# A transformer layer with a state-space mixer on one core: the down projection as seven block products, with tokens on partitions

## The chip, the cores and the metric

The kernel runs on 1 core of a Trainium2 chip. TensorE (PE) multiplies, VectorE (DVE), ScalarE (ACT) and GpSimd (POOL) work on vectors, and the DMA queues of SyncE (SP), ACT and POOL move data. The metric is the device time of one execution in microseconds.

## The reference

One layer over 512 latent tokens and 256 context tokens of width 1024, all in float32. In this change only the end of the layer matters. Written with the names of the reference:

```python
out_lat = (g_ssd * (y_ssd @ w_o_ssd) + g_att * (y_att @ w_o_att)) @ w_out   # 1024 x 1024
x = x + gate1 * out_lat                       # gate1, gate2: of the six modulation vectors
h = rmsnorm(x, norm2_g) * (1 + scale2) + shift2
u = dwconv_centred(h @ w_up, conv_w, conv_b)  # 1024 x 5632, taps over 3 tokens
a, b = u[..., :2816], u[..., 2816:]
x = x + gate2 * ((silu(a) * b) @ w_down)      # 2816 x 1024
out = rmsnorm(x, final_g)
```

The six modulation vectors of 1024 come from `silu(c) @ w_mod + b_mod`.

## The kernel before

Every large product is made of three: each operand is split into a high part in the format that PE takes at full rate (`hi`, a cast on ACT, L148) and the rest (`lo`, a subtraction on DVE, L149), and PE adds hi x hi, hi x lo and lo x hi into one bank of PSUM (`gemm`, L186, products L192, L193, L195). Channels lie on partitions throughout: a weight block of 128 x 128 is the stationary operand, and 512 tokens stream past it. One "piece" is eight such blocks, 128 x 1024, 512 KB.

`run` (L166) takes the program as a list of steps with the pieces that each needs, and emits the load and split of a piece one step ahead of its use. Loads go through three raw buffers on the SP queue; split pieces have two buffers (`whi`, `wlo`). Where an output tile has only eight blocks of inputs, one piece is 24 products.

The order of instructions on each engine is drawn up when the kernel is built, from the program's order and from when an instruction's operands are expected; where `manual_schedule` names PE, PE keeps the order as written. An instruction waits in its queue until its operands are there, and all behind it wait too. DMAs that are ready early can be put far ahead of the step that they belong to.

The stages at the end, in order:

- Merge, `os_step` (L1549), eight output tiles of 48 products; the gated sum is split into `mh` and `ml`. Ten of the 32 steps `m_step` (L540) are woven in: each takes a 512 KB piece of `w_mod`, scales it by the conditioning vector on DVE (L553) and adds; after four, PE turns the sum of four column groups onto partitions (L557) and DVE reduces it into `mod2` (L559). Six more lie in the next stage, eight in the up stage.
- W_out, `out_step` (L1618) and `out_last` (L1632): eight output tiles of 24 products. The residual is added with the gate as a value per partition (L1627) and squares are added for the second norm. The last three tiles are done in halves of 256 tokens, so that the root (`half_root`, L1602; its power runs on POOL, L246) and its spreading over the partitions by PE (`rms_spread`, L249) lie beside products.
- Up, `up_step` (L1706): 22 steps of two output tiles, 48 products each. The first is done in token halves, after `norm2_k` (L1661). ACT and DVE make the convolution and the gate; the result is split into `fh` and `fl` (L1697, L1698).
- Down, `down_step` (L1743) and `down_last` (L1754): eight output tiles of 66 products over three pieces; the last tile in halves, with the sums of the final norm between them. The final scaling and the stores to `out`, channels first, end the kernel; the host transposes.

Of the kernel before, what the change touches and what calls it, by code (L numbers as in the profile page):

```python
# [44 lines left out]
def tile_hybrid_layer(  # L45
# [26 lines left out]
    sel_d: bass.AP,  # L72
    out: bass.AP,
# [12 lines left out]
    def psum_pools(**sizes):  # L86

        if banks_:
            banks_["s"].close()
        s = banks_["s"] = ExitStack()  # L90
        for name, (n, w) in sizes.items():
            pool = s.enter_context(tc.tile_pool(name="p" + name, bufs=n, space=PSUM, reuse_waits="tile"))
            banks_[name] = pool, w

    def bank(name):
        pool, w = banks_[name]
        return pool.tile([P, 512 * w], F32, tag=name, name=name)
# [8 lines left out]
    def accb():  # L106
        return bank("acc")
# [15 lines left out]
    for i in range(8):  # L123
# [5 lines left out]
        for u, n in ((0, 8), (1, 8), (2, 6)):  # L129
            src["dn", 3 * i + u] = wdn[i, :, u * 1024 : u * 1024 + n * P], n * P  # L130
# [409 lines left out]
    def m_step(i):  # L540
        cg, kk = i // 4, i % 4

        def fn(r):
# [10 lines left out]
            if kk == 3:  # L554
# [7 lines left out]
        return [("m", i)], fn  # L562
# [997 lines left out]
    x1 = [hpool.tile([P, 4, L], F32, tag=t, name="x1") for t in ("hch", "hcl")]  # L1560
    q2 = hpool.tile([P, L], F32, name="q2")
    g1h = cpool.tile([P, 8], F32, name="g1h")
    a2 = cpool.tile([P, 8], F32, name="a2")

# [3 lines left out]
    HL = L // 2  # L1568
    HALF = [slice(0, HL), slice(HL, L)]

    def add_square(q, x, o):
        if o == 0:
            S.activation(q, x, AF.Square)
        else:
            sq = tmp("tc")
            S.activation(sq, x, AF.Square)
            V.tensor_tensor(q, q, sq, ALU.add)

    def half_gemm(ps, xh, xl, z, w, m, k0, nk, after={}):

        wh, wl = w
        for k in range(m):
            n, c = k0 + k, slice(k * P, (k + 1) * P)
            h, l = xh[:, n, z], xl[:, n, z]
            T.matmul(ps[:, :HL], wh[:, c], h, start=n == 0, stop=False)
            T.matmul(ps[:, :HL], wh[:, c], l, start=False, stop=False)
            T.matmul(ps[:, :HL], wl[:, c], h, start=False, stop=n == nk - 1)
            if n in after:
                after[n]()

    def half_sums(pf, q, u):

        rms_sums(pf[:, 2 * u : 2 * u + 2], q[:, HALF[u]], 2, 0, u == 0, False)

    def half_squares(parts):
        r = []
        for n, x in enumerate(parts):
            r.append(tmp("te" if n > 1 else "tc")[:, :HL])
            S.activation(r[-1], x, AF.Square)
        return r  # L1600

    def half_root(pf, sqs, u):  # L1602
        for n, sq in enumerate(sqs):
            rms_sums(pf[:, 2 * u : 2 * u + 2], sq, 2, 0, False, n == len(sqs) - 1)
        return rms_root(pf[:, 2 * u : 2 * u + 2], 2, EPS)
# [7 lines left out]


    for o in (5, 6, 7):
        ELSEWHERE["out", o] = piece_in("yh%d" % (o - 5))

    def out_step(o):  # L1618
        def fn(w):
            xt = tmp("te")  # L1620
            nc.sync.dma_start(xt, xT[o // 2, :, (o % 2) * L : (o % 2 + 1) * L])
            ps = accb()
            gemm([(ps, mh, ml)], w)
            if o == 0:
                V.tensor_scalar_mul(g1h, mod2[:, 0:8], 0.5)
            xo = x1[o // 4][:, o % 4, :]
            V.scalar_tensor_tensor(xo, ps, g1h[:, o : o + 1], xt, ALU.mult, ALU.add)  # L1627
            add_square(q2, xo, o)

        return [("out", o)], fn  # L1630

    def out_last(*w):  # L1632
        xt = [cp.tile([P, L], F32, tag="ld", name="ld", bufs=3) for _ in range(3)]
        for i, o in enumerate((5, 6, 7)):
            nc.sync.dma_start(xt[i], xT[o // 2, :, (o % 2) * L : (o % 2 + 1) * L])
        pf = F["pf"] = misb()
        F["r2"] = []

        def root():
            F["rs2"] = half_root(pf, F["sq2"], 0)  # L1640

        def spread():
            F["r2"].append(rms_spread(F["rs2"], 2))

        with tc.manual_schedule(engines={mybir.EngineType.PE}):
            for u, z in enumerate(HALF):
                for i in range(3):
                    after = {}
                    if u == 1:
                        after = {0: {5: root}, 1: {4: spread}}.get(i, {})  # L1650
                    if i == 2:
                        after[2] = lambda u=u: half_sums(pf, q2, u)
                    ps = accb()
                    half_gemm(ps, mh, ml, z, w[i], 8, 0, 8, after)
                    x = x1[1][:, 1 + i, z]
                    V.scalar_tensor_tensor(x, ps[:, :HL], g1h[:, 5 + i : 6 + i], xt[i][:, z], ALU.mult, ALU.add)
# [249 lines left out]
```

## Time and profile before

Three runs took 1264.0, 1267.4 and 1268.2 us: a median of 1267.44. The profiled execution has a span of 1266.2 us from its first to its last instruction; its time beside the span is not listed.

| engine | busy, us | share | instructions |
|---|---|---|---|
| PE (products) | 1241.7 | 98% | 6418 |
| DVE | 871.2 | 69% | 1413 |
| ACT | 653.0 | 52% | 1221 |
| POOL | 137.5 | 11% | 113 |

Busy time of an engine is the time in which one of its instructions runs. Products on PE overlap, so the duration listed for one (0.39 us at 512 columns) is longer than the distance from one to the next. "Idle before" is the time that an engine stood still ahead of an instruction, with what ended it. Rows of DMA issues give the size and the time from issue to landing.

### The profile page before, as it was taken

How to read it: one execution, taken by the hardware profiler on the slowest of the kernel's cores; microseconds unless marked ns; L12 is line 12 of the kernel's file. 1: busy time of each engine (PE TensorE's matmuls, PEld its weight loads, DVE VectorE, ACT ScalarE, POOL GpSimd, SP SyncE). 2: the span in 40 equal slices, each digit the busy share in tenths (PEclk: the TensorE clock that was granted, in tenths of full speed). 3: DMA queues.
4: the chain of work that ended last, by engine and by line, in shares of the span. 5: the costliest groups of instructions: out<-in, count | busy, mean ns of one | idle time of the engine just before them, and what ended most of it. 6: DMA issues, size and time to landing. Idle time of an engine off the chain costs nothing.

```text
span 1266.2 us, 17234 instructions
## 1 busy us (share of the span) xinstructions
PE 1241.7 (98%) x6418; PEld 1025.9 (81%) x6418; DVE 871.2 (69%) x1413; ACT 653.0 (52%) x1221; POOL 137.5 (11%) x113
## 2 busy tenths in 40 slices
PE   7999999999999999999999999999999999999997
PEld 4698888888888778788777777889988888888886
DVE  3856887888655687877887676676777777773333
ACT  3557788877445466475674653223644444442221
POOL 0000000000000142251352530000200000000000
PEclk9999999999999999999999999999999999999998
DMA  8652242222355225345355567776233333332331
GB/s 328 245 163 86 63 133 72 88 79 76 115 161 172 92 84 150 126 136 172 109 142 175 182 218 254 235 240 200 67 115 109 125 102 115 117 112 92 99 97 67
DMA packets 90419, 174.55 MB, mean 138 GB/s; under 512 B 7648, under 2 KB 43296, under 8 KB 90336
## 3 DMA queue, kind: packets, MB, share of 16 engines
q1 hardware_dynamic: 89248, 172.41, 42.6%
q8 instruction: 50, 0.82, 0.3%
q10 hardware_dynamic: 1088, 1.05, 0.2%
q14 instruction: 33, 0.27, 0.1%
HBM read 150.82 MB, written 17.11 MB: 133 GB/s over the span
## 4 chain that ended last, share of the span: by engine, by line
PE 84%; DVE 7%; POOL 3%; ACT 2%; DMA 2%; issue 1%; SPq 0%; DVEq 0%; ACTq 0%; POOLq 0%
PE acc L195 20%; PE acc L192 20%; PE acc L193 20%; PE score L777 3%; PE po L826 3%; PE pt L813 2%; PE mis L405 2%; PE mis L1420 1%; PE mis L1414 1%; PE acc L896 1%; PE acc L898 1%; PE acc L897 1%; POOL dx L1426 1%; DVE wlo L149 1%; PE acc L1715 1%
## 5 line engine op out<-in xcount | busy, mean ns | idle before, releaser
L149 DVE TENSOR_TENSOR wlo<-wraw,whi 128x1024 fp32r<-128x1024 f32 (+1 forms) x129 | 162.4, 1259 | 122.3 <-ACT whi L148 119.0
L148 ACT CAST whi<-wraw 128x1024 fp32r<-128x1024 f32 (+1 forms) x129 | 133.1, 1034 | 185.4 <-PE acc L193 138.4
L192 PE MATMUL acc<-hlh,whi 128*128 128x512 f32 x488 | 200.1, 410 | 0.0
L195 PE MATMUL acc<-hlh,wlo 128*128 128x512 f32 x488 | 191.3, 392 | 0.0
L193 PE MATMUL acc<-hll,whi 128*128 128x512 f32 x488 | 190.9, 391 | 0.0
L192 PE MATMUL acc<-mh,whi 128*128 128x512 f32 x368 | 143.4, 390 | 0.0
L195 PE MATMUL acc<-mh,wlo 128*128 128x512 f32 x368 | 143.2, 389 | 0.0
L193 PE MATMUL acc<-ml,whi 128*128 128x512 f32 x368 | 143.2, 389 | 0.0
L195 PEld LDWEIGHTS acc<-hlh,wlo 128*128 128x128 f32 x488 | 91.6, 188 | 20.1
L193 PEld LDWEIGHTS acc<-hll,whi 128*128 128x128 f32 x488 | 91.9, 188 | 18.1 <-issue 2.4
L192 PEld LDWEIGHTS acc<-hlh,whi 128*128 128x128 f32 x488 | 91.9, 188 | 17.8 <-issue 2.4
L195 PEld LDWEIGHTS acc<-mh,wlo 128*128 128x128 f32 x368 | 69.1, 188 | 14.5
L193 PEld LDWEIGHTS acc<-ml,whi 128*128 128x128 f32 x368 | 69.1, 188 | 14.3
L192 PEld LDWEIGHTS acc<-mh,whi 128*128 128x128 f32 x368 | 69.1, 188 | 14.1
L1325 POOL TENSOR_TENSOR st<-st,eT 128x512 f32<-128x512 f32 x24 | 28.3, 1179 | 449.3 <-ACT st L1342 430.3
L246 POOL TENSOR_TENSOR rs<-ms,phalf 128x2 f32<-128x2 f32 (+1 forms) x7 | 7.4, 1051 | 543.0 <-DVE ms L245 543.0
L786 DVE CUSTOM_DVE_ANT_0 p<-score,winm,nsink 128x512 f32<-128x512 f32 (+1 forms) x64 | 51.8, 810 | 15.5 <-PE score L777 14.0
L192 PE MATMUL acc<-fh,whi 128*128 128x512 f32 x154 | 60.0, 390 | 0.0
L195 PE MATMUL acc<-fh,wlo 128*128 128x512 f32 x154 | 59.9, 389 | 0.0
L193 PE MATMUL acc<-fl,whi 128*128 128x512 f32 x154 | 59.9, 389 | 0.0
L793 ACT ACTIVATE p<-p,mneg 128x512 f32<-128x512 f32 (+1 forms) x64 | 49.7, 777 | 15.4 <-DVE mneg L786 14.8
L1207 DVE SCALAR_TENSOR_TENSOR ta<-acc,half,ta 128x511 f32<-128x511 f32 (+1 forms) x66 | 43.8, 663 | 19.6 <-ACT ta L1206 19.6
(362 smaller groups left out, 2863.5 us busy)
## 6 DMA issues: line engine op xcount, KB each, us to landing
wraw<-wup SPq DMA_DIRECT2D x44, 512.0 KB, 3.5
fb<-cs_d SPq DMA_DIRECT2D x32, 512.0 KB, 5.9
wraw<-wm SPq DMA_DIRECT2D x32, 512.0 KB, 3.6
wraw<-wx SPq DMA_DIRECT2D x24, 512.0 KB, 3.6
wm<-wm SPq DMA_DIRECT2D x16, 512.0 KB, 8.2
wraw<-wz SPq DMA_DIRECT2D x16, 512.0 KB, 3.5
wraw<-wos SPq DMA_DIRECT2D x16, 512.0 KB, 4.2
wraw<-wdn SPq DMA_DIRECT2D x16, 512.0 KB, 3.5
```

The lines of the kernel that those rows point to most:

```text
L148: S.copy(hi[:, :n], r[:, :n])
L149: V.tensor_tensor(lo[:, :n], r[:, :n], raw(hi[:, :n]), ALU.subtract)
L192: T.matmul(ps, wh, xh[:, k0 + k, :], start=a, stop=False)
L193: T.matmul(ps, wh, xl[:, k0 + k, :], start=False, stop=False)
L195: T.matmul(ps, wl, xh[:, k0 + k, :], start=False, stop=b)
L405: T.matmul(pg[i], w[a][:, i * P : (i + 1) * P], h[b], start=st and a + b == 0, stop=en and a == 1, skip_group_check=True,)
L777: T.matmul(ps[:, o : o + len(z) * P], Q[h][:, b * P : (b + 1) * P], k[:, j, z[0] * P : (z[-1] + 1) * P], start=v == 0 and o % 512 in (0, P ...
L786: V.tensor_tensor_reduce(p[:, :w], d["ps"][i][:, o0 : o0 + w], m, op0=ALU.add, op1=ALU.min, scale=1.0, scalar=nsink[:, h : h + 1], accum_o ...
L793: S.activation(p, p, AF.Exp, bias=d["mneg"][:, i : i + 1], scale=-1.0, accum_out=d["den"][:, i : i + 1])
L826: T.matmul(d["po"], vst[:, cols[x], j, :], d[y][x], start=x == 0 and y == "pth", stop=x == c - 1 and y == "ptl")
L1207: V.scalar_tensor_tensor(o[:, 1:n], ps[:, 0 : n - 1], hcol(base_w, i), o[:, 1:n], ALU.mult, ALU.add)
L1325: G.tensor_tensor(h8(n), h8(s), bc64(eT[:, z0 : z0 + 8, c]), ALU.mult)
```

## The change

The down projection becomes Strassen's method in Winograd's form on blocks of two: tokens in two halves of 256, the 2816 input channels in alternate tiles of 128 (11 pairs), the 1024 output channels in halves of 512. Seven block products take the place of eight. Each is three products per pair and token tile, now with the activations as the stationary operand and 512 output channels streaming, so the result has tokens on partitions. The inner dimension goes in two chunks, six pairs and then five.

- The sums of activations (`s3`, `r2`, `s4`, and one in place) are made on POOL by `pair_sums`, four operations of 256 columns for each pair: the first six pairs in the up stage, the other five within the down stage.
- The sums of weights are made by accumulating DMAs from POOL's queue, onto the raw piece once it has been split (`NEXT_SUM`), 24 of full or half pieces.
- Weights are split in each block product; the activations too, one pair of low halves on POOL for each on DVE. Results are saved from PSUM by ACT (`snap`), combined on DVE, multiplied by the gate, and added to the residual on POOL.
- W_out runs the same way round: all eight pieces for token tiles 0 and 1, then for 2 and 3, kept split in the buffers of the mixer's output. The gate is multiplied into the W_out piece on POOL before its split. The x rows are loaded by token into the buffers of the residual.
- Both later norms sum squares by ACT's accumulation, with the root as a value per partition. For the up projection PE turns the normed rows back (`turned`).
- The gate vectors are needed along the free dimension: their four groups are summed over partitions by a product with ones. The order of the groups is changed, and 16 of the `m_step`s lie in merge steps 2 to 6, none in the W_out stage.
- PSUM becomes one pool of eight banks from W_out on.
- The output is stored with tokens first, and the host no longer transposes.

```diff
+        if key[0] == "out":
+            G.tensor_tensor(r, r, F["g1"], ALU.mult)
...
-        cg, kk = i // 4, i % 4
+        cg, kk = (2, 3, 4, 5, 0, 1, 6, 7)[i // 4], i % 4
...
+            if kk == 3 and cg in (0, 1, 6, 7):
+                ps = misb()
+                T.matmul(ps, ones, acc, start=True, stop=True)
+                g = F["g1" if cg < 2 else "g2"][:, 512 * (cg % 2) : 512 * (cg % 2) + 512]
+                V.tensor_tensor(g, ps, g, ALU.add)
...
+    def square_sum(ss, t, c):
+        junk = tmp("tm")
+        S.activation(junk, x1_of(t, c), AF.Square, accum_out=ss[:, t, c : c + 1])
+
+    def root(ss, t):
...
+        V.tensor_tensor(ms, ss[:, t, 0:1], ss[:, t, 1:2], ALU.add)
+        V.tensor_scalar(ms, ms, 1.0 / D, EPS, ALU.mult, ALU.add)
+        G.tensor_tensor(rs, ms, phalf[:, 0:1], ALU.pow)
...
+    def out_products(k, ts, w):
+        for a, xs_ in ((0, mh), (1, mh), (0, ml)):
+            for t in ts:
+                for c in range(2):
+                    T.matmul(F["o", t, c], xs_[:, k, tok(t)], w[a][:, CH[c]], start=k == a == 0 and xs_ is mh, stop=k == 7 and xs_ is ml)
+
+    def out_done(t):
+        for c in range(2):
+            V.tensor_tensor(x1_of(t, c), x1_of(t, c), F["o", t, c], ALU.add)
+            square_sum(ss2, t, c)
+        rs = root(ss2, t)
...
+            S.activation(xr, x1_of(t, c), AF.Copy, scale=rs)
...
+    def norm2(banks, r, k):
+        src_, z = banks[k // 2][:, (k % 2) * HL : (k % 2 + 1) * HL], HALF[r]
+        a, s = a2[:, k : k + 1], mod2[:, 8 + k : 9 + k]
+        S.activation(h2h[:, k, z], src_, AF.Identity, scale=a, bias=s)
+        u = tmp("tb" if k % 2 else "ta")[:, :HL]
+        V.tensor_scalar(u, src_, a, s, ALU.mult, ALU.add)
+        (G if k % 2 else V).tensor_tensor(h2l[:, k, z], u, raw(h2h[:, k, z]), ALU.subtract)
+
+    def out_last():
+        for t in range(2):
+            out_done(t)
+        F.update({("o", t, c): accb() for t in (2, 3) for c in range(2)})
         with tc.manual_schedule(engines={mybir.EngineType.PE}):
+            for k in range(KT):
+                out_products(k, (2, 3), F["wo", k])
+                if k == 4:
+                    banks = turned(0)
+            for k in range(KT):
+                norm2(banks, 0, k)
+        for t in (2, 3):
+            out_done(t)
...
+        s3, r2, s4 = (c2.tile([P, HL], F32, tag=n, name=n, bufs=6) for n in ("s3", "r2", "s4"))
+        G.tensor_tensor(s3, a11, a21, ALU.subtract)
+        G.tensor_tensor(r2, s3, a22, ALU.add)
+        G.tensor_tensor(s4, a12, r2, ALU.subtract)
+        G.tensor_tensor(a21, a21, a22, ALU.subtract)
...
-        V.tensor_tensor(a, a, b, ALU.mult)
-        S.copy(F["h"][:, t, :], a)
-        V.tensor_tensor(F["l"][:, t, :], a, raw(F["h"][:, t, :]), ALU.subtract)
+        V.tensor_tensor(F["a", t], a, b, ALU.mult)
+        if t % 2 and t < 12:
+            pair_sums(t // 2)
...
+    NEXT_SUM = {"p3": ("p7", 1), "p7": ("p6", 0), "p6": ("p4", 2), "p1": ("p5", 1)}
...
+        def prepared(name, g):
+            n = 512 * len(pairs(g))
+            w = dn["w", SLOT[name], g]
+            hi = wpool.tile([P, 1024], F32R, tag="whi", name="whi", bufs=2)
+            lo = wpool.tile([P, 1024], F32R, tag="wlo", name="wlo", bufs=2)
+            split(w, n, hi, lo)
+            if name in NEXT_SUM:
+                nc.gpsimd.dma_start(w[:, :n], wdn[NEXT_SUM[name][1], g, :, :n], accum_op=ALU.add)
+            a = []
+            for j, p in enumerate(pairs(g)):
+                ah, al = (c2.tile([P, HL], F32R, tag=t_, name=t_, bufs=8) for t_ in ("ah", "al"))
+                x = F["A", p][name]
+                if name == "p1":
+                    S.activation(ah, x, AF.Copy, scale=-1.0)
+                    V.scalar_tensor_tensor(al, x, -1.0, raw(ah), ALU.mult, ALU.subtract)
+                else:
+                    S.copy(ah, x)
+                    (V if j else G).tensor_tensor(al, x, raw(ah), ALU.subtract)
...
+        def product(name, chunk, bank, first, last):
...
+                for j, (ah, al) in enumerate(a):
+                    z = slice(512 * j, 512 * j + 512)
+                    for t in range(2):
...
+                        T.matmul(bank[t], ah[:, tok(t)], hi[:, z], start=st, stop=False, skip_group_check=True)
+                        T.matmul(bank[t], al[:, tok(t)], hi[:, z], start=False, stop=False, skip_group_check=True)
+                        T.matmul(bank[t], ah[:, tok(t)], lo[:, z], start=False, stop=en, skip_group_check=True)
...
+        def update(r, c, t, y, eng=None):
+            V.tensor_tensor(y, y, F["g2"][:, CH[c]], ALU.mult)
+            (eng or G).tensor_tensor(x1_of(2 * r + t, c), x1_of(2 * r + t, c), y, ALU.add)
+
+        def finish(t):
+            rs, y = root(ss3, t), {}
+            for c in range(2):
+                V.scalar_tensor_tensor(x1_of(t, c), x1_of(t, c), rs, F["fg"][:, CH[c]], ALU.mult, ALU.mult)
+                (S if c else nc.sync).dma_start(out[t * P : (t + 1) * P, CH[c]], x1_of(t, c))
...
+                product("p3", chunk, f_, True, True)
+                f = snap(f_, "ta")
+                product("p1", chunk, m, True, True)
+                sa = snap(m, "tb")
+                product("p7", chunk, h, True, True)
+                hs = snap(h, "tc")
+                product("p6", chunk, m, False, True)
+                sb = snap(m, "te")
+                product("p2", chunk, e, True, True)
+                for t in range(2):
+                    V.tensor_tensor(sa[t], e[t], sa[t], ALU.subtract)
+                    update(0, 0, t, sa[t])
+                if not end:
+                    load_w(1, "p3")
+                    for p in range(6, PAIRS):
+                        pair_sums(p)
+                product("p5", chunk, m, False, True)
+                for t in range(2):
+                    V.tensor_tensor(f[t], m[t], f[t], ALU.add)
+                    update(0, 1, t, f[t])
+                    V.tensor_tensor(hs[t], m[t], hs[t], ALU.subtract)
+                    update(1, 1, t, hs[t])
...
+                product("p4", chunk, h, False, True)
+                for t in range(2):
+                    V.tensor_tensor(sb[t], h[t], sb[t], ALU.subtract)
+                    update(1, 0, t, sb[t], V if end else G)
...
-        + weave([os_step(o) for o in range(2, 8)], msteps[8:18])
-        + weave([out_step(o) for o in range(5)], msteps[18:24])
+        + [([], load_x), ([], open_g1)]
+        + weave([os_step(o) for o in range(2, 7)], msteps[8:24])
+        + [os_step(7)]
```

More of the change, by code (lines that the diff above doesn't have):

```diff
@@ L72, in tile_hybrid_layer @@
     sel_d: bass.AP,
+    xn: bass.AP,
+    bm: bass.AP,
+    fg: bass.AP,
     out: bass.AP,
@@ L1579, in half_gemm @@
[L1579 to L1605, printed above, removed]
+    def one_pool():
+        psum_pools(acc=(8, 1))
+        banks_["mis"] = banks_["acc"]
@@ L1607, in piece_in, with open_g1, load_x @@
+    def open_g1():
+        F["g1"] = cp.tile([P, D], F32, name="g1")
+        nc.sync.dma_start(F["g1"], bm[0].partition_broadcast(P))
+    def load_x():
+        for t in range(4):
+            nc.sync.dma_start(x1[t // 2][:, t % 2, :], xn[t])
     def piece_in(tag):
@@ L1632, in out_last @@
[L1632 to L1643, printed above, removed]
-        with tc.manual_schedule(engines={mybir.EngineType.PE}):
[L1646 to L1656, printed above, removed]
-                F["sq2"] = half_squares([x1[1][:, 1 + i, z] for i in range(3)])
@@ new lines, in out_step, with turned @@
+    def out_step(k):
+        def fn(w):
+            F["wo", k] = w
+            if k == 0:
+                F.update({("o", t, c): accb() for t in range(2) for c in range(2)})
+            out_products(k, (0, 1), w)
+        return [("out", k)], fn
+    def turned(r):
+        banks = [accb() for _ in range(4)]
+        for t in (2 * r, 2 * r + 1):
+            for k in range(KT):
+                c0 = (k % 2) * HL + (t % 2) * P
+                T.transpose(banks[k // 2][:, c0 : c0 + P], F["xr", t, k // 4][:, (k % 4) * P : (k % 4 + 1) * P], ident)
+        return banks
@@ L1683, in up_first @@
+    def up_first(pa, t):
         a = tmp("ta")
@@ L1707, in fn @@
         def fn(wa, wb):
-            pa, pb = accb(), accb()
             if t == 0:
```

256 lines of the change are left out of this document (128 added, 128 removed).

## The prediction

> **What bounds the kernel now.** I read the shares first, then the chain that ended last, then busy time by stage.
>
> ```profile
> span 1266.2 us, 17234 instructions
> PE 1241.7 (98%) x6418; PEld 1025.9 (81%) x6418; DVE 871.2 (69%) x1413; ACT 653.0 (52%) x1221; POOL 137.5 (11%) x113
> PE 84%; DVE 7%; POOL 3%; ACT 2%; DMA 2%; issue 1%; SPq 0%; DVEq 0%; ACTq 0%; POOLq 0%
> ```
>
> TensorE is both the busiest engine and the chain. The table by stage (columns: stretch, length, busy time and count of PE, PEld, DVE, ACT, POOL, then clock, DMA share, GB/s) cuts the part that the change touches. Its rows are the merge steps 2 to 7, the W_out projection, the first up step, the other up steps, the down projection, and the tail:
>
> ```profile
> 777.50:842.80 65.30, 65.30 (x293) 54.02 (x292) 47.19 (x66) 15.88 (x18) 0.00 (x0) 1.00 0.75 249
> 842.80:890.70 47.90, 47.90 (x296) 43.04 (x295) 33.85 (x52) 17.63 (x27) 1.92 (x3) 1.00 0.61 194
> 890.70:904.20 13.50, 13.50 (x112) 13.12 (x111) 8.96 (x20) 8.84 (x21) 6.27 (x8) 1.00 0.11 39
> 904.20:1133.20 229.00, 229.00 (x1014) 189.59 (x1014) 166.10 (x210) 100.05 (x128) 0.00 (x0) 1.00 0.35 115
> 1133.20:1256.30 123.10, 122.97 (x613) 104.55 (x611) 40.51 (x48) 29.17 (x35) 0.70 (x1) 1.00 0.26 78
> 1256.30:1266.20 9.90, 1.68 (x8) 1.20 (x8) 4.59 (x13) 0.79 (x2) 2.11 (x3) 0.66 0.60 212
> ```
>
> PE never pauses from 777.5 to 1256.3, and DVE and POOL are nearly free in the down stage. The up row gives the pitch: 21 steps of 48 products are 1008 in 229.0 us less two transposed m groups (0.7, below), so 0.2265; consecutive starts below give 0.227. I use 0.2267.
>
> **Part by part.** *TensorE in the down stage.* Before, 528 products of 512 columns (the last output tile in halves) take 123.1 us with their sums. Strassen's seven need 7 x 66 = 462: 252 in the first chunk (six pairs), 57.1 us, and 210 in the second (five), 47.6: together 104.7, a gain of 18.4 if nothing waits.
>
> *What feeds them.* Each weight piece is still cast on ACT and subtracted on DVE, but now serves 12 products (2.72 us), or 6 (1.36) for the odd pair, where it served 24 (5.4). There are 42 such pieces where there were 24, and the activations, cast once before, are cast in each product.
>
> ```profile
> 1100.37 0.39 PE L195 MATMUL acc<-mh,wlo 128*128 128x512 f32 x1
> 1100.57 1.05 ACT L148 CAST whi<-wraw 128x1024 fp32r<-128x1024 f32 x1 [0.38 <-PE acc L193]
> 1100.60 0.39 PE L192 MATMUL acc<-mh,whi 128*128 128x512 f32 x1
> 1100.83 0.39 PE L193 MATMUL acc<-ml,whi 128*128 128x512 f32 x1
> 1101.66 1.23 DVE L149 TENSOR_TENSOR wlo<-wraw,whi 128x1024 fp32r<-128x1024 f32 x1 [0.74 <-ACT whi L148]
> L149 DVE TENSOR_TENSOR wlo<-wraw,whi 128x1024 fp32r<-128x1024 f32 x71 | 86.9, 1223 | 71.0 <-ACT whi L148 70.1
> L1516 DVE TENSOR_TENSOR tb<-tb,ld 128x512 f32<-128x512 f32 x8 | 5.5, 684 | 0.1
> L1671 DVE SCALAR_TENSOR_TENSOR ml<-tb,mod,mh x8: 475/484/485, 887.5 to 902.0; 128x256 fp32r<-128x256 f32 x8
> L1669 POOL TENSOR_TENSOR ml<-ta,mh x8: 724/736/742, 888.4 to 902.9; 128x256 fp32r<-128x256 f32 x8
> 740.75 2.48 DVE L1446 TENSOR_TENSOR zs<-mis,zs 128x512 f32<-128x512 f32 x4 [0.97 <-PE mis L1445]
> ```
>
> A buffer freed at 1100.6 has its low half at 1102.89, 2.29 later (2.36 with the release). There are two buffers, and the low half is needed at the third product of the next piece: 2.72 + 0.45 = 3.17, so it fits. Behind an odd pair it is 1.36 + 0.45 = 1.81: 0.55 late, at each of the second chunk's six product borders. The DVE work that follows a product is earlier in the program than the next splits; I assume that it goes first. After p5 that is eight operations, started 0.5 before the border and 0.6 apart (L1446: 2.48/4), to 4.3 after it; the split then ends at 5.5: 2.4 late in the first chunk, 5.0 in the second. After p2 (four) it is about 1.5 late in the second. Latency therefore costs 2.4, and 4 x 0.55 + 1.5 + 5.0 = 8.7.
>
> *DVE against POOL.* POOL gets the low halves of every first pair, the pair sums and the residual additions. One place in this trace has both engines dense, each reading two SBUF operands:
>
> ```profile
> 742.24 6.92 POOL L1304 TENSOR_TENSOR ssq<-ssq,sq 128x512 f32<-128x512 f32 x4 [3.19 <-ACT sq L1301]
> 744.61 5.10 DVE L1494 SCALAR_TENSOR_TENSOR yl<-ta,vec,yh 128x512 fp32r<-128x512 f32 x3
> L1494 DVE SCALAR_TENSOR_TENSOR yl<-ld,vec,yh x13: 740/746/752, 750.8 to 764.1; 128x512 fp32r<-128x512 f32 x13
> L1494 DVE SCALAR_TENSOR_TENSOR yl<-ta,vec,yh x3: 1721/1759/1776, 744.6 to 748.0; 128x512 fp32r<-128x512 f32 x3
> L1427 POOL TENSOR_TENSOR dx<-dx,te x16: 1282/1361/2158, 457.7 to 737.8; 128x512 f32<-128x512 f32 x16
> ```
>
> The same DVE line takes 0.746 alone and 1.76 beside POOL: the two take turns, one of each in 5.10/3 = 1.70, where their own durations make 1.28 + 0.746 = 2.03. I charge each 0.15 less than alone. First chunk: POOL 38 x 0.585 (18 low halves, 20 pair sums) + 8 x 1.13 = 31.2; DVE 21 x 1.07 + 24 x 0.33 + 8 x 0.54 (splits, low halves, gate products) = 34.7; together 65.9, which is 8.8 over TensorE's 57.1. Second chunk: POOL 18 x 0.585 + 6 x 1.13 = 17.3; DVE 14 x 1.07 + 7 x 0.54 + 17 x 0.33 + 6 x 0.54 + 4 x 0.54 = 29.6; 46.9, just within 47.6, so there latency rules. The down stage is 65.9 + 2.4 + 47.6 + 8.7 = 124.6: 1.5 more than before. Ends: no taking turns and splits first, 104.7 + 6 x 0.55 = 108.0 (-15.1); whole durations in turn, POOL 38.2 and DVE 42.8, then 20.9 and 37.2, 81.0 + 2.4 + 58.1 + 8.7 = 150.2 (+27.1). I take the middle, as the row with both dense measures it.
>
> The Trainium skill (SBUF — State Buffer, "SBUF: two separate sides") says that the pair of ports shared by DVE and GpSimd is an exclusive lock, held for the whole instruction. By that rule the sum is the upper end; the 1.70 against 2.03 is a little kinder.
>
> *Accumulating DMAs.* POOL issues 24, forming the next block's weights in place; the trace has none.
>
> ```profile
> wraw<-wdn SPq DMA_DIRECT2D x16, 512.0 KB, 3.5
> wraw<-wos SPq DMA_DIRECT2D x9, 512.0 KB, 4.8
> xsb<-xT SPq DMA_DIRECT2D x4, 512.0 KB, 8.8
> L1621 SPq DMA_DIRECT2D te<-xT x5: 328/328/332, 737.7 to 860.6; - x5
> L553 DVE SCALAR_TENSOR_TENSOR tm<-wraw,csil,tm 128x512 f32<-128x512 f32 x56 | 42.7, 762 | 13.3 <-DMA wraw<-wm 12.6
> ```
>
> The tightest is p7 to p6: a piece is free 2.3 after its cast and cast again one product later, leaving 8.2 - 2.3 = 5.9, or 4.5 in the second chunk. At 3.5 to 4.5 it is hidden, at 8.8 it costs 2.9 + 4.3 = 7.2; nothing can be gained. I take 0, by the quiet stage's 3.5. Behind an issue that waits for the split, POOL's low halves queue; eight buffers, four pieces ahead, cover that. Issuing takes 24 x 0.33 = 8 of POOL's time by L1621's row (the last row serves below). The Trainium skill (DMA: Bandwidth & Descriptors, "Anatomy of one DMA") prices the GpSimd path at 2.0 us plus bytes over 436 GB/s, an estimate of 3.2 here without the addition; by it the term stays 0.
>
> *W_out and the second norm.*
>
> ```profile
> 656.42 1.72 PE mis L1414 x4
> 1133.24 0.60 PE L557 MATMUL mis<-ident,tm 128*128 128x128 f32 x4
> 1133.60 0.48 PE L192 MATMUL acc<-fh,whi 128*128 128x512 f32 x1
> ```
>
> Before: 47.9 + 13.5 = 61.4. After: 192 x 0.2267 = 43.5, 32 transposes at 0.36/4 = 2.9, and 96 half-width products at 0.12 (13.5/112) = 11.5: 57.9. The norm chain of the last two token tiles (adds, squares, root, two scalings, transposes, first split: some 8 us) has the 5.8 us of the first half of the up step over it and the transposes: 2 late. POOL's 1024-wide gate product (2 x 1.13) and DVE's split share a port, 3.4 a piece, 27 us for eight, against 21.8 of products plus some 8 of head start: 2 late at the end of the head start. So 61.9, +0.5; ends -3.5 and +8.
>
> *Mod columns.* Four groups are summed by a product with ones at 1.72/2 = 0.86 instead of four transposes at 0.36 together: 4 x 0.5 = +2.0.
>
> *Merge stage.* 16 mod pieces instead of 10 go beside it, 3 MB more on 16.3 MB: share 0.75 becomes 0.89; the x rows (2.1 MB) may go earlier, as L1621 does 100 us ahead of its use, or raise it to 0.98. Loads queue in order on SP, so a merge weight waits behind them; DVE rises by 12 x 0.76 = 9 of 65.3 and stays free. Between 0 and 21.3 MB at 249 GB/s = 85.5 (+20): I take 3, as a share of 0.89 still fits and a piece has about 2 us of slack. *Up stage:* it loses a copy and a subtraction and gains POOL sums with room beside them: 0, between -0 and +2.
>
> *Tail.*
>
> ```profile
> 1256.34 0.48 DVE L1791 SCALAR_TENSOR_TENSOR x<-acc,mod,x 128x256 f32<-128x256 f32 x1
> 1258.59 0.69 POOL L246 TENSOR_TENSOR rs<-ms,phalf 128x2 f32<-128x2 f32 x1 [5.29 <-DVE ms L245]
> ```
>
> Six DVE operations, two squares, root, four scalings and the store replace a similar chain with two TensorE passes: some 10 us for 9.9, so 0.
>
> Sum: 1.5 + 0.5 + 2.0 + 3 + 0 = +7.0 on the span of 1266.2, 1273.2. The median of the runs shown is 1.2 above that span: 1274.
>
> **Rivals.** *Faster, 1259:* the port is no bound. Low halves run four pieces ahead, so taking turns costs only where POOL's operations meet a split. It decides if a 256-wide POOL operation holds the port under (57.1 - 34.7 - 9.0)/38 = 0.35 us. Then the down stage is 104.7 + 2.4 + 8.7 = 115.8 (-7.3) or 108.0 (-15.1), with +2.5 and no merge loss: 1263 to 1255. Against it: the 1.76 us row. *Whole-instruction turns, 1300:* +27.1 + 5.5. Against: the 1.70.
> The Trainium skill's lock rule (SBUF — State Buffer, "SBUF: two separate sides") gives this end too.
>  *Accumulation lands late, 1281:* +7.2; only if it is as slow as the starting loads. *Merge stage DMA-bound, 1284:* +10 more. *No net change:* the terms cancel within 0.3%, about what a measurement of this kernel can tell from no change.
>
> **Numbers.** Forecast 0.40; faster rival 0.27; whole turns 0.10; late accumulation 0.08; merge 0.05; within 0.3% 0.10. Slower in all 0.63, faster 0.27. The range runs from the fast rival's better end to just under the slow one, 1255 to 1299; the forecast's own is 1268 to 1284.
>
> **What would show it.** Down-stage products 462; its length near 125 us with PE pauses after p5 of some 2 and 5 us and at the second chunk's borders of 0.5; DVE splits and POOL operations well over 1.22 and 0.74 in mean; POOL above half busy there. Wrong: PE dense through the first chunk, or POOL at its own durations; pauses waiting on a DMA; pauses before 843.

## The result and the profile after

The changed kernel takes 1309.4 us (median of 4, 1307.8 to 1311.8) against 1266.9 for the kernel before: a ratio of 1.034, 95% interval 1.0325 to 1.0362. It is 43 us slower; 1274 was forecast, with 1299 as the upper end.

The shares, from the page of the kernel after:

```profile
span 1308.8 us, 17079 instructions
PE 1244.7 (95%) x6180; PEld 1010.3 (77%) x6180; DVE 940.6 (72%) x1465; ACT 691.4 (53%) x1319; POOL 274.1 (21%) x241
...
DVE 2%; PE 2%; issue 1%; POOL 1%; DMA 1%; ACT 0%; POOLq 0%; DVEq 0%; ACTq 0%
```

PE has 238 instructions fewer, yet is 3 us longer busy, and idle for 64.1 us where it was for 24.5. The chain that ended last can be followed back over 7% of the span only, so the stages and the waits have to tell. The table by stage of the kernel after (columns as in the prediction; rows: merge steps 2 to 7, W_out to the end of the second up step, the other up steps, down, tail):

```profile
774.85:857.60 82.75, 73.80 (x301) 56.48 (x300) 59.90 (x85) 16.08 (x18) 7.21 (x3) 0.96 0.71 234
857.60:934.85 77.25, 73.37 (x369) 61.91 (x368) 46.60 (x66) 34.36 (x59) 24.09 (x19) 0.96 0.31 102
934.85:1153.80 218.95, 218.95 (x964) 180.78 (x963) 145.59 (x180) 83.67 (x109) 20.14 (x27) 1.00 0.36 114
1153.80:1297.60 143.80, 118.12 (x464) 90.98 (x462) 113.42 (x118) 75.65 (x139) 94.41 (x92) 0.92 0.62 136
1297.60:1308.80 11.20, 0.03 (x1) 0.00 (x0) 6.53 (x14) 1.44 (x4) 1.10 (x2) 0.65 0.24 94
```

The second row ends one up step later than two of the rows of before do, because two up steps interlace now; before, the same stretch is 47.9 + 13.5 + 229.0/21 = 72.3.

| stretch | before | forecast | after | difference |
|---|---|---|---|---|
| up to merge step 2 | 777.5 | 0 | 774.85 | -2.6 |
| merge 2 to 7 | 65.3 | +3 | 82.75 | +17.4 |
| W_out, first two up steps | 72.3 | +0.5 | 77.25 | +5.0 |
| other up steps | 218.1 | (mod columns +2) | 218.95 | +0.9 |
| down | 123.1 | +1.5 | 143.8 | +20.7 |
| tail | 9.9 | 0 | 11.2 | +1.3 |

Together +42.7. In the runs below that leave the steps ahead of it as they are, the first row ends between 772.8 and 776.4 where it was read. The granted clock, 1.00 in all of before's rows but the tail, is 0.92 in the down stage.

What PE waited for there (total, times, longest):

```profile
PE acc L1821 <- DVE wlo L150: 14.7, 11, 5.2
PE acc L1821 <- DVE mt L1599: 7.3, 1, 7.3
PE acc L1819 <- ACT whi L149: 3.6, 2, 2.9
```

From the starts of the 462 products I separate three parts: 104.7 of work at 0.2267 apiece, 27.7 of pauses (distances over 0.6, less the pitch), and 10.5 more for products at some 0.43 apiece, while the clock stood at half behind a pause. By chunk, the pauses and the slowed products take 20.8 in the first and 18.2 in the second, where 11.2 (8.8 + 2.4) and 8.7 were forecast. Two of four 2 us windows, inside and behind the pause at p4 of the first chunk:

```profile
1222.00:1224.00 2.00, 0.00 (x0) 0.00 (x0) 2.00 (x1) 0.00 (x0) 2.00 (x2) 0.62 0.00 0
1226.00:1228.00 2.00, 2.00 (x6) 1.54 (x5) 2.00 (x3) 0.41 (x1) 1.82 (x2) 0.50 0.70 250
```

Six products in 2 us where 8.8 are usual.

The block products run in the order p3, p1, p7, p6, p2, p5, p4 in each chunk. The first long pauses, at p7 and p6 of the first, in the timeline of the kernel after (start, duration):

```profile
1173.51 0.87 POOL L1796 DMA_DIRECT2D dnw<-wdn  x1
1174.12 1.72 POOL L1700 TENSOR_TENSOR s<-fa 128x256 f32<-128x256 f32 x2
1174.38 4.58 DVE L150 TENSOR_TENSOR wlo<-wraw,whi 128x1024 fp32r<-128x1024 f32 x1 [0.54 <-ACT whi L149]
1175.51 1.69 POOL L1703 TENSOR_TENSOR fa<-fa 128x256 f32<-128x256 f32 x2
1176.89 0.98 POOL L1806 TENSOR_TENSOR al<-r,ah 128x256 fp32r<-128x256 f32 x1
1177.55 1.16 POOL L1796 DMA_DIRECT2D wraw<-wdn  x1
1183.37 1.04 ACT L149 CAST whi<-wraw 128x1024 fp32r<-128x1024 f32 x1 [8.03 <-DMA wraw<-wdn]
```

A split of 1.22 takes 4.58 beside five POOL operations in a row. The accumulating DMA that p6 needs stands behind those operations in POOL's queue (7 us behind its split), and lands 5.8 after its issue: two causes for the pause at p6.

### The profile page after: what moved, and what is told of

Read it like the earlier page. It is cut to its first block, busy times and chain, and to the rows that moved or that the text cites. A ratio compares the mean times of both kernels' runs of the same rounds, so it can differ in the third digit from the quotient of the medians.

```text
span 1308.8 us, 17079 instructions
## 1 busy us (share of the span) xinstructions
PE 1244.7 (95%) x6180; PEld 1010.3 (77%) x6180; DVE 940.6 (72%) x1465; ACT 691.4 (53%) x1319; POOL 274.1 (21%) x241
## 5 line engine op out<-in xcount | busy, mean ns | idle before, releaser
L150 DVE TENSOR_TENSOR wlo<-wraw,whi 128x1024 fp32r<-128x1024 f32 (+2 forms) x117 | 157.8, 1349 | 86.2 <-ACT whi L149 82.4
L149 ACT CAST whi<-wraw 128x1024 fp32r<-128x1024 f32 (+2 forms) x117 | 121.5, 1040 | 157.4 <-PE acc L196 79.5
L195 PE MATMUL acc<-mh,whi 128*128 128x512 f32 x328 | 128.0, 390 | 0.0
L198 PE MATMUL acc<-mh,wlo 128*128 128x512 f32 x328 | 127.6, 389 | 0.0
L196 PE MATMUL acc<-ml,whi 128*128 128x512 f32 x328 | 127.6, 389 | 0.0
L1821 PE MATMUL acc<-wlo,ah 128*128 128x512 f32 x154 | 65.0, 422 | 22.1 <-DVE wlo L150 14.7
L195 PEld LDWEIGHTS acc<-mh,whi 128*128 128x128 f32 x328 | 61.6, 188 | 13.1 <-issue 0.2
L1819 PE MATMUL acc<-whi,ah 128*128 128x512 f32 x154 | 63.7, 414 | 3.6 <-ACT whi L149 3.6
L796 DVE CUSTOM_DVE_ANT_0 p<-score,winm,nsink 128x512 f32<-128x512 f32 (+1 forms) x64 | 51.9, 811 | 15.5 <-PE score L787 14.0
L1820 PE MATMUL acc<-whi,al 128*128 128x512 f32 x154 | 62.9, 408 | 0.0
L1216 ACT ACTIVATE ta<-acc,half 128x512 f32<-128x512 f32 (+1 forms) x66 | 46.6, 706 | 22.2 <-PE acc L198 18.5
```

The costliest lines, as they stand in the source:

```text
L149: S.copy(hi[:, :n], r[:, :n])
L150: V.tensor_tensor(lo[:, :n], r[:, :n], raw(hi[:, :n]), ALU.subtract)
L195: T.matmul(ps, wh, xh[:, k0 + k, :], start=a, stop=False)
L196: T.matmul(ps, wh, xl[:, k0 + k, :], start=False, stop=False)
L198: T.matmul(ps, wl, xh[:, k0 + k, :], start=False, stop=b)
L796: V.tensor_tensor_reduce(p[:, :w], d["ps"][i][:, o0 : o0 + w], m, op0=ALU.add, op1=ALU.min, scale=1.0, scalar=nsink[:, h : h + 1], accum_o ...
```

## The experiments

I call the operations that combine and add a block product's result its posts. Theories for the down stage: **queue** (what stands ahead of a split in DVE's queue), **port** (POOL holds what DVE needs), **DMA** (the accumulating transfers are slow); for the merge stage, buffers against bandwidth. Down stage of each run in us, from the starts of its products:

| run | down | pauses | slowed clock |
|---|---|---|---|
| after | 143.6 | 27.7 | 10.5 |
| e1 posts behind splits | 132.8 | 20.3 | 7.1 |
| e2 without the late pair sums | 140.3 | 24.7 | 10.2 |
| e3 without accumulation | 138.1 | 22.9 | 9.8 |
| e4 low halves on DVE | 140.0 | 25.5 | 9.0 |
| e5 nothing but issues on POOL | 136.7 | 23.8 | 7.8 |
| e9 p2 ahead of p6 | 140.1 | 26.9 | 7.9 |
| e8 posts behind splits, low halves and additions on DVE | 129.0 | 17.3 | 6.3 |
| e11, e12 (all three: posts, POOL, p2 ahead) | 116.1, 116.2 | 7.5 | 3.5 |

Three runs that leave the down stage as it is have it at 143.3 (e10), 144.4 (e7) and 146.0 (e6). So a difference of some 3 us says little by itself; which pauses go and which stay says more.

**e1: posts behind the splits.**

```diff
-                product("p4", chunk, h, False, True)
+                product("p4", chunk, h, False, True, {1: [lambda: post_m(0)], 2: [lambda: post_m(1)]})
...
+                for fn in after.get(g - gs[0], ()):
+                    fn()
```

> The combining operations that follow a block product (subtract or add, multiply by the gate, add to the residual) are put behind the splits of the second piece of the next product, those of the second token tile behind the third piece; the final norm of token tiles 0 and 1 is put behind the last product. Nothing is left out. Queue theory (the pauses come from what stands ahead of a split in DVE's queue): the pauses of the changed kernel at p5 and p4 of the first chunk and at p3, p1, p5 and p4 of the second (1.9, 5.4, 1.2, 1.2, 0.9 and 7.5 us, with 6.5 us of slowed clock behind them, 24.6 together) mostly go: down stage 122 to 127 in place of 143.4, kernel 1287 to 1293. Port theory (DVE's operations are long because POOL holds the port): the same operations still run beside POOL's additions, so about half stays: down stage 131 to 136. DMA theory (the accumulating transfers are too slow): hardly any change, 140 or more.

Down 132.8: short of what the queue theory asked (122 to 127), and within the port theory's range (131 to 136). Kernel 1304.6, ratio 1.0297 (1.0280 to 1.0314), where 1287 to 1293 was expected. Counted from a product's start to the next one's, p4 of the first chunk lost 1.6 us where it lost 7.9, and p4 of the second 1.5 for 10.4. But the displaced posts now meet p3 and p1 of the second chunk (4.0 and 5.7 for 1.4 and 1.3), and the tail grew by 6.0. Stage table of e1, down and tail:

```profile
1150.04:1282.85 132.81, 114.85 (x464) 87.96 (x462) 107.27 (x109) 74.12 (x134) 85.79 (x89) 0.96 0.63 139
1282.85:1300.00 17.15, 0.17 (x1) 0.00 (x0) 11.41 (x24) 3.28 (x10) 4.22 (x6) 0.61 0.32 122
```

So the pauses do follow the posts, as the queue theory has it, and of some 16 us won by moving them 13 are given back later, in the second chunk and the tail. The wait of 7.3 that the profile puts down to the norm's `mt` was mostly theirs. DVE in the kernel after, ahead of the last product's first splits:

```profile
1279.89 0.68 DVE L1869 TENSOR_TENSOR ta<-acc,ta 128x512 f32<-128x512 f32 x1
...
1285.19 0.68 DVE L1832 TENSOR_TENSOR tc<-tc,g 128x512 f32<-128x512 f32 x1
1285.80 1.22 DVE L1598 TENSOR_TENSOR mt<-ss 128x1 f32<-128x1 f32 x1
1286.93 1.21 DVE L150 TENSOR_TENSOR wlo<-dnw,whi 128x1024 fp32r<-128x1024 f32 x1
```

Posts from 1279.89 to 1285.8, then the norm for 1.1. At p4 of the first chunk the eight posts are followed by two stretched splits:

```profile
1216.00 0.68 DVE L1869 TENSOR_TENSOR ta<-acc,ta 128x512 f32<-128x512 f32 x1
...
1220.19 1.75 DVE L1832 TENSOR_TENSOR tc<-tc,g 128x512 f32<-128x512 f32 x1
1221.86 4.49 DVE L150 TENSOR_TENSOR wlo<-wraw,whi 128x1024 fp32r<-128x1024 f32 x2
```

**e2, e3: without the late pair sums; without accumulation.**

```diff
-                    for p in range(6, PAIRS):
-                        pair_sums(p)
...
-                x = F["A", p][name]
+                x = F["A", p if p < 6 else p - 6][name]
```

```diff
-            if name in NEXT_SUM:
+            if False:
```

> Leaves out the activation sums of the last five pairs (20 POOL operations in the first chunk): the second chunk takes the sums of the first five pairs in their place. Port theory and POOL-queue theory: the pauses at p7 (2.5 us) and p6 (3.0 and 1.5, with 2.5 of slowed clock) of the first chunk go, down stage 143.4 to about 134; the first accumulating transfers from p7 to p6 are issued within 2 us of their split where it was 7. DMA theory: the landing alone is too long (5.8 us in a window of 5.9), so a pause of 1 to 3 us stays at p6; down stage 137 to 141. DVE-queue theory alone: no change at p7, as nothing on DVE moves.

> Leaves out the accumulating DMAs: a block product takes the weights that stand in its buffer without the next block added. DMA theory: the pauses at p6 of both chunks (4.5 and 1.6, slowed clock 2.5 and 0.9, together 9.5) go: down stage about 134. Port theory: the pause at p7 (2.5) and those at p5 and p4 stay as they are, and the pause at p6 gets no shorter than 1.5, as the split there took 2.06 beside POOL. Queue theory: as DMA theory at p6, for the issues stand behind pair sums in POOL's queue; p4 and p5 stay.

e2, without the late sums: 140.3, in the DMA theory's range. The pause inside p7 goes, as the port and POOL's queue have it; PE still waits 2.2 for the transfer at p6, and p4 loses only 1.7 less. e3, with weights that lack the next block: 138.1, where the DMA theory asked for about 134. The waits for a transfer go in both chunks, but p6 of the first still waits 2.7, now for a low half made on POOL behind pair sums. Each theory holds a part, and neither part alone explains the stage. The transfers in the kernel after (KB each, median us from issue to landing):

```profile
dnw<-wdn POOLq DMA_DIRECT2D x11, 512.0 KB, 6.0
wraw<-wdn POOLq DMA_DIRECT2D x9, 512.0 KB, 5.8
dnw<-wdn SPq DMA_DIRECT2D x10, 512.0 KB, 7.0
wraw<-wdn SPq DMA_DIRECT2D x2, 512.0 KB, 3.4
```

Accumulating takes 6.0, where I had assumed 3.5, and where two plain loads issued apart take 3.4. The ten plain loads at 7.0 are no measure of one transfer, as six were issued together at the start of the stage and landed after 4.8 to 17.1. The estimate of 3.2 from the Trainium skill (DMA: Bandwidth & Descriptors, "Anatomy of one DMA") has no term for the addition, and the measurement decides.

**e4, e5: low halves on DVE; all elementwise work on DVE.**

```diff
-                    (V if j else G).tensor_tensor(al, x, raw(ah), ALU.subtract)
+                    V.tensor_tensor(al, x, raw(ah), ALU.subtract)
...
-                        pair_sums(p)
+                        pair_sums(p, V)
...
-            (eng or G).tensor_tensor(x1_of(2 * r + t, c), x1_of(2 * r + t, c), y, ALU.add)
+            V.tensor_tensor(x1_of(2 * r + t, c), x1_of(2 * r + t, c), y, ALU.add)
```

(e4 has the first edit alone.)

> All low halves of the activations on DVE, none on POOL. Port theory: 33 operations of about 1.0 us leave POOL, DVE's splits fall towards 1.22 us and its low halves to 0.42; DVE takes 33 x 0.42 = 14 us more but loses more than that by shorter operations: down stage 125 to 133. Queue theory: the pauses at the borders stay, as the posts still stand ahead of the splits and POOL's additions and pair sums still run: 140 to 148.

> Down stage with no elementwise work on POOL: low halves, the pair sums of the last five pairs and the residual additions on DVE; POOL keeps the issues of the accumulating DMAs and the roots. Nothing is left out, and DVE has some 49 + 36 x ... operations more: 34 low halves and 20 sums of about 0.35 us and 14 additions of about 0.62, 27.6 us together. Port theory: DVE's operations fall to their own durations (split 1.2, low half 0.38), which gives back more than the 27.6; the pauses at p7 and p6 of the first chunk go, those behind the posts stay: down stage 122 to 132 in place of 143.4. Queue theory without the port: DVE's queue only gets longer, 145 to 160.

e4 gives back only 3.6. That is the number that the queue theory asked for (140 to 148) and not the port theory's 125 to 133, but its timeline shows the port:

```profile
1166.55 0.88 POOL L1796 DMA_DIRECT2D dnw<-wdn  x1 [1.39 <-DVE wlo L150]
1166.84 4.50 DVE L150 TENSOR_TENSOR wlo<-wraw,whi 128x1024 fp32r<-128x1024 f32 x1
1167.17 1.71 POOL L1700 TENSOR_TENSOR s<-fa 128x256 f32<-128x256 f32 x2
1168.55 1.70 POOL L1703 TENSOR_TENSOR fa<-fa 128x256 f32<-128x256 f32 x2
```

With its low halves gone, POOL runs four sums back to back, and the split stands still for all four: 4.50 - 1.22 = 3.28, for 3.08 from the start of the first to the end of the last. This happens four times. The Trainium skill (SBUF — State Buffer, "Who interferes with whom") says that a DVE instruction with two SBUF inputs contends with a GpSimd instruction that reads SBUF, and that the shared pair of ports is an exclusive lock. The trace agrees, and shows more than that: between two POOL instructions the split did not get its turn (4.50 for one of 1.22).

In e5 the splits are back at their own duration. Groups of the down stage (busy, mean ns), of the kernel after:

```profile
L150 DVE TENSOR_TENSOR wlo<-dnw,whi 128x1024 fp32r<-128x1024 f32 (+1 forms) x27 | 36.6, 1362 | 15.5 <-ACT whi L149 15.5
L150 DVE TENSOR_TENSOR wlo<-wraw,whi 128x1024 fp32r<-128x1024 f32 (+1 forms) x14 | 24.0, 1717 | 10.1 <-ACT whi L149 8.7 <-PE acc L559 1.3
```

and of e5:

```profile
L150 DVE TENSOR_TENSOR wlo<-dnw,whi 128x1024 fp32r<-128x1024 f32 (+1 forms) x27 | 29.6, 1103 | 14.6 <-ACT whi L149 14.6
L150 DVE TENSOR_TENSOR wlo<-wraw,whi 128x1024 fp32r<-128x1024 f32 (+1 forms) x14 | 16.5, 1182 | 8.7 <-ACT whi L149 7.4 <-PE acc L559 1.3
```

DVE does 67 operations more and is busy for 106.7 us instead of 113.4. The stage falls by 6.9 only, to 136.7, between the two ranges expected: the port's stretching is gone, but the posts still stand ahead of the splits (5.0 at p4, 7.5 at the last product) and p6 waits 2.2 for its transfer.

**e9: a longer window for the transfers.**

```diff
-                product("p6", chunk, m, False, True)
-                sb = snap(m, "te")
...
+                product("p6", chunk, m, False, True)
+                sb = snap(m, "te")
                 product("p5", chunk, m, False, True)
```

> The changed kernel with block product p2 put ahead of p6, and nothing else: the accumulating transfers from p7 to p6 then have a whole product more before their piece is cast, and those from p6 to p4 one less (one stays). Nothing is left out. DMA theory (issue to landing takes 6 to 9 us, the window was 5.9): the pauses at p6 (4.2 us lost in the first chunk, 1.9 in the second) go, those at p7, p5 and p4 stay: down stage 137 to 140 in place of 143.6. Port theory: p6 keeps what its split loses beside POOL, 1 to 2 us, and p2 now meets the pair sums: 139 to 144.

140.1. PE no longer waits for a transfer at p6, so the window was too short. In its place the posts of p2 now meet a split at p6 (2.1), and four low halves in a row on POOL meet two splits at p5 (2.5), which neither theory had said. The total is at the upper end of the DMA theory's range; the pause that is gone is the evidence for it.

**e6, e7, e10: merge stage and W_out.**

```diff
+        if key[0] == "m" and key[1] in MERGE_M:
+            r = cp.tile([P, 1024], F32, tag="wm2", name="wm2", bufs=2)
...
+                for _ in range(4):
+                    accb()
```

```diff
-        + weave([os_step(o) for o in range(2, 7)], msteps[8:24])
+        + weave([os_step(o) for o in range(2, 8)], msteps[8:18])
...
+        + weave([out_step(k) for k in range(KT)], msteps[18:24])
```

```diff
-        if key[0] == "out":
-            G.tensor_tensor(r, r, F["g1"], ALU.mult)
```

> Two edits in stages apart. The mod pieces of the merge steps get two buffers of their own in place of a share of the three raw buffers; and W_out's sums begin in four other banks of PSUM than those that the merge steps used last. Nothing is left out. Merge, buffer theory (loads wait on SP for a free raw buffer, 51 us of 83): the stage falls from 82.7 to 66 to 71 us. Bandwidth theory (19.4 MB at the 249 GB/s of before): 77 to 83. W_out to the end of the second up step, bank theory (the wait of 3.0 us for the last merge step's read of its bank, and 2.9 of slowed clock behind it): 77.3 falls to 71 to 72.5; if the wait is for the merge result itself, 76 to 77.5.

> The mod pieces as they were spread before the change: ten in the merge steps, six in the W_out steps, with the groups that W_out's gate needs first. Nothing is left out. If the six pieces more are what the merge stage lost: it falls from 82.7 to 65 to 68 us; the W_out stage takes six loads and nine DVE operations more, 0 to 4 us longer than 77.3 to the end of the second up step. If the stage is long for another reason (x rows, the gate's product on POOL): 76 or more.

> Leaves out the gate of the first residual: W_out's pieces are not multiplied by it on POOL. Queue theory for W_out's wait (the last merge step's read of PSUM stands on DVE behind the split of a W_out piece, which waits for cast, gate product and load in turn): the wait of 3.0 us at the fourth product of W_out falls to under 1.5, the slowed clock behind it (2.9) goes, and the stretch to the end of the second up step falls from 77.3 to 71.5 to 74. If the load alone holds the split, the wait stays at 2 to 4 and the stretch at 76 or more. The down stage is not touched, 143 to 145.

What SP waited for in the merge stage of the kernel after:

```profile
SPq L145 <- DVE wlo L150: 26.0, 13, 6.5
SPq L145 <- DVE tm L556: 25.2, 16, 4.2
```

For 51 of 83 us the next load waits until DVE has freed one of three buffers. The merge row of e6, with two more:

```profile
775.80:847.84 72.04, 68.69 (x301) 55.34 (x300) 57.85 (x85) 16.37 (x18) 4.67 (x2) 1.00 0.77 264
```

72.0 at 264 GB/s with the same bytes, a little above the 66 to 71 of the buffer theory and under the 77 to 83 of the bandwidth theory. The buffers cost 10.7 of the 17.4; what holds the other 6.7 was not tried apart. In e7 (merge, then W_out) the six pieces only move their price:

```profile
776.40:844.26 67.86, 67.44 (x293) 54.74 (x292) 48.55 (x68) 16.34 (x18) 4.21 (x2) 1.00 0.74 238
844.26:936.98 92.72, 79.25 (x378) 64.18 (x377) 57.20 (x84) 34.53 (x59) 24.27 (x20) 0.93 0.37 119
```

Merge gives back 14.9, W_out takes 15.5, since all eight pieces of W_out are needed in its first 22 us: PE waits there 7.3 us for their casts and 2.3 for their splits. I expected 0 to 4 there: a miss.

In e6 the fourth product of W_out still waited for the last merge step (5.5 us, where it was 3.0): asking for four banks ahead did not help (78.8 for the stretch, 71 to 72.5 expected), and the trace does not show which banks it gave. e10 shows what holds it. DVE in the kernel after, and PE's wait:

```profile
859.59 1.22 DVE L150 TENSOR_TENSOR wlast<-wraw,wlast 128x1024 fp32r<-128x1024 f32 x1 [3.36 <-ACT wlast L149]
860.73 0.68 DVE L1525 TENSOR_TENSOR tb<-acc,ld 128x512 f32<-128x512 f32 x1
...
861.47 0.79 PE L1625 MATMUL acc<-whi,mh 128*128 128x512 f32 x1 [3.03 <-DVE tb L1525]
```

The merge step's read of PSUM stands behind the split of a W_out piece, which waits for its cast, and that for the gate product on POOL. Without the gate, the stretch is 71.5, the wait is gone, and the clock is 1.00:

```profile
855.90:927.40 71.50, 70.55 (x369) 59.88 (x368) 38.48 (x65) 33.28 (x58) 8.85 (x13) 1.00 0.31 103
```

**e8, e11, e12: together.** Diffs as above; e12 multiplies the gate into the sums on DVE and moves four mod pieces ahead into the mixer's steps.

```diff
-            V.tensor_tensor(x1_of(t, c), x1_of(t, c), F["o", t, c], ALU.add)
+            V.tensor_tensor(y, F["o", t, c], F["g1"][:, CH[c]], ALU.mult)
+            V.tensor_tensor(x1_of(t, c), x1_of(t, c), y, ALU.add)
...
-        m = msteps[2 * g : 2 * g + 2]
+        m = msteps[3 * g : 3 * g + 3]
```

> Together: nothing but issues on POOL in the down stage, the posts behind the second and third pieces' splits, the mod pieces spread as before the change, W_out's sums in other banks. Nothing is left out. Port and queue theory together: down stage 112 to 120, merge 65 to 68, W_out to second up step 71 to 76, tail 11 to 17: kernel 1258 to 1275. If a third cause holds the down stage (the accumulating transfers), 1275 to 1290.

> All that the runs so far point to, nothing left out: in the down stage POOL only issues (low halves, pair sums of the last five pairs and residual additions on DVE), the posts behind the second and third pieces' splits, p2 ahead of p6, the last tokens' sums ahead of the final norm on DVE; in the merge steps two buffers for the mod pieces. Port, queue and DMA theory together: down stage 113 to 121, merge 70 to 73, tail 13 to 16, W_out as it was: kernel 1270 to 1281. If DVE is now the bound of the first chunk (some 62 us of work in 57.1 of products), 121 to 127 and 1280 to 1288.

> The kernel of the run before (POOL only issues in the down stage, posts behind splits, p2 ahead of p6, two buffers for the mod pieces), and besides: the first residual's gate multiplied on DVE into the sums of W_out in place of the weights, four mod pieces moved from the merge steps into the mixer's steps ahead of them, and the four roots of the final norm ahead of its scalings on DVE. Nothing is left out. Queue theory: W_out to the end of the second up step falls from 79.7 to 71.5 to 75 (the wait of 5.5 goes, two multiplications for each of the last tokens come into the norm's chain), merge from 73.8 to 67 to 70, tail 15.9 to 14 to 15.5, down stage as it was, 114 to 118: kernel 1263 to 1270, which is no more than before. If the mod pieces cost as much in the mixer's steps as in the merge steps: 1268 to 1275.

e8 took 1297.8 (ratio 1.0244, 1.0227 to 1.0261), a miss: its late pair sums stayed on POOL, against what the expectation says. POOL is 35.5 us busy there where e5's was 21.9, and p1, p7 and p6 of the first chunk lost 11.1 us where they had lost 9.9. So it is a test of the posts, with low halves and additions on DVE and the sums on POOL: 129.0.

e11 took 1276.8 (ratio 1.0069, 1.0052 to 1.0086), as expected, with the down stage at 116.1; its merge row (73.8) and W_out row (79.7) came out higher than expected. Its down row, and all that PE waited for there:

```profile
1147.15:1263.25 116.10, 110.33 (x464) 86.91 (x462) 101.17 (x174) 74.47 (x135) 19.80 (x23) 0.99 0.70 159
```

```profile
PE acc L1828 <- DVE wlo L154: 2.8, 5, 0.8
PE acc L1827 <- DVE al L1811: 2.3, 1, 2.3
PE acc L1826 <- ACT te L1834: 0.5, 1, 0.5
```

With the three causes removed the stage falls by 27.5, more than the 21.2 of e1, e5 and e9 taken one by one. Strassen's products then beat the eight by 7.0 of the 18.4 us within the stage; but posts have moved into the tail, which is 15.9 long, so that stage and tail together gain 1.0. e12 took 1274.7 (ratio 1.0054, 1.0037 to 1.0071), which is the range given for mod pieces that cost as much in the mixer's steps as in the merge steps: against e11 the merge row falls by 3.2, and the start of it comes 3.8 later. Its rows for merge, W_out and tail:

```profile
778.50:849.10 70.60, 68.18 (x298) 55.08 (x298) 52.97 (x76) 17.32 (x20) 0.00 (x0) 1.00 0.73 244
849.10:923.90 74.80, 72.21 (x369) 61.09 (x368) 43.13 (x73) 33.40 (x58) 9.62 (x13) 0.98 0.30 97
...
1259.10:1274.10 15.00, 0.16 (x1) 0.00 (x0) 11.48 (x25) 2.89 (x8) 2.74 (x4) 0.65 0.36 140
```

Against before these are +5.3, +2.5 and +5.1: more than the 6.9 won in the down stage. No version tried beats the kernel before.

## Why the prediction was wrong

Of the +42.7, against +7.0 forecast, the down stage has 20.7 (1.5 forecast) and the merge steps 17.4 (3 forecast). The terms one by one:

- **TensorE, -18.4:** right. The 462 products are there, and dense stretches run at the pitch taken (0.228).
- **Latency, 2.4 + 8.7:** the mechanism was right, the posts' size was not. p4 of the first chunk paused 5.4 (2.4 forecast), the last product 7.5 (5.0), p5 of the first chunk 1.9 (nothing); the odd pair's 0.55 came out as 0.53 at p7 of the second chunk. The step that failed is "0.6 apart": beside POOL's additions the eight posts took 5.9 where 4.8 was assumed, the split behind them took 2.3 in the first chunk where 1.2 was, and in the second the norm's 1.1 stood there too, which the sum did not have. e5 does not part these: its pause at p4 stays at 5.0, as the additions now stand in DVE's queue themselves.
- **DVE against POOL, +8.8:** near in size (e5 gives back 6.9, after what the 67 operations more cost DVE), wrong in kind; that the size came near is in part luck. I compared sums of busy time and chose turns at 1.70 for a pair. What counted was when: a split caught by a row of POOL operations stands still for all of them (e4). "POOL above half busy" and stretched splits were seen. (The second chunk's sum adds up to 47.1, not 46.9, and stays within 47.6.)
- **Accumulating DMAs, 0:** failed at "I take 0, by the quiet stage's 3.5". Landing takes 6.0 in a window of 5.9, and the issue itself stood 7 us behind pair sums; I had looked at what waits behind an issue, not at what an issue waits behind. Worth some 3.5 to 5.5 (e9, e3), where the rival had 7.2. An issue held POOL for 0.86 to 1.2, not for the 0.33 taken from an SP row, so that issues made up nearly all of POOL's 21.9 in e5.
- **The clock:** left out altogether. 10.5 us in the down stage, some 3 in the merge steps, 2.9 in W_out. Every pause was priced at its own length.
- **Merge, +3:** failed at "a piece has about 2 us of slack", which went by shares of bandwidth. It came to +17.4: the loads waited for one of three buffers, and two buffers more gave back 10.7 (e6). The rest stays open. The rival named the stage and not the reason.
- **W_out, +0.5:** failed at "2 late at the end of the head start". The gate's lateness blocked an older read in DVE's queue: 3.0, with 2.9 of slowed clock.
- **Mod columns, tail:** +0.9 and +1.3 for +2.0 and 0; right within 1.3.
- **The range:** its top took one upper end at a time. Down, merge and W_out came out towards their upper ends together (+20.7, +17.4 and +5.0, for +27.1, +20 and +8). That these share a cause, more small steps through few buffers and the same queues, is my reading, and no run tests it.

## What to carry to other kernels

Fewer products pay only if what feeds them shrinks too; here each piece served half as many products and brought more operations. Price a step by what stands ahead of it in each engine's queue and by how many buffers its loads have, at the moment it is needed, and not by the sum of busy time in its stage. Add the slowed clock to a pause of a few us (here up to 2.9 us behind one), and ask whether upper ends can come together.

## What the runs showed of the hardware

- A split (128x1024, 1.22 us alone) beside four POOL operations of 256 columns back to back took 4.48 to 4.50 us, three times in e4, and 4.14 once.
- Behind the pauses of 5.4 and 7.5 us in the down stage, and behind 3.0 and 1.5 close together, 12 to 14 products ran at 0.43 us: 2.5 to 2.9 more. A pause of 2.5 that stood by itself cost 0.1 more, one of 1.9 cost 0.5. The Trainium skill (TensorE: Matmul & The Clock Gate, "Part 1: The HAM clock gate") has the clock at half after an idle window of about 3.4 us, free-running; the granted 0.50 agrees, and here shorter pauses were enough at times: in e4 nine slowed products followed a pause of 2.1.
- An accumulating DMA of 512 KB landed 5.8 to 6.0 us after its issue in the median (5.3 to 10.2 over all), and its issue held POOL for 0.86 to 1.2 us.
